# A MoE block's down projection with stationary weights, and three of twelve low parts made on GpSimd

## Chip, core and metric

The kernel runs on one core of one Trainium2 chip. The metric is the device time of one execution in microseconds, the median of three runs. The engines are called as the profile calls them: PE is TensorE's matmul, PEld its weight load, DVE is VectorE, ACT is ScalarE, POOL is GpSimd, and SP is the engine that issues most of the DMAs.

## What is computed

A decoder block over 512 tokens of width 1024: a gated linear recurrence and a sliding-window attention side by side, then a mixture of 32 experts of which every token takes four. The change touches the mixture alone. All is float32, and the weights of all 32 experts are read once, 12 MiB for each.

```python
def moe_ffn(h, w_router, b_router, w_up, b_up, w_down, b_down):
    logits = xf @ w_router + b_router
    top_vals, top_idx = lax.top_k(logits, 4)
    gates = softmax(top_vals)
    ...
    def expert_block(args):                    # xb: the tokens of one expert
        hu = xb @ w_up[e] + b_up[e]            # 1024 -> 2048
        x_glu = jnp.minimum(hu[:, ::2], 7.0)
        x_lin = jnp.clip(hu[:, 1::2], -7.0, 7.0)
        act = x_glu * sigmoid(1.702 * x_glu) * (x_lin + 1.0)
        return act @ w_down[e] + b_down[e]     # 1024 -> 1024
    ...                                        # times the gate, added to the token's row
```

## The kernel before

**Float32 by halves.** A float32 weight is cut into a float16 high part and a float16 low part, and so are the activations; a product is the sum of three float16 passes (high by high, high by low, low by high: `PASSES`). `split` does the cutting for one chunk of weights, 1 MiB as [128, 2048] float32: ACT writes the high part (line 344, a scaled copy), DVE writes the low part in one instruction (line 345: source times scale minus high part, both inputs in SBUF).

**One expert.** Up to C = 96 token slots are gathered into `xg` (`pick`), transposed, by matmuls with a one-hot matrix. The up projection takes eight chunks (`up_k`, line 1141): the weights are stationary, the 96 slots move, 48 matmuls to a chunk, into four PSUM banks `pu`. `swiglu` on DVE and ACT makes the activations in two halves: the first as float16 high and low parts (`act`), the second as float32 (`act32`). The down projection takes four chunks (`down_j`): here the activations are stationary and the weights move, 512 columns at a time, into two PSUM banks `pd`. Chunks 0 and 1 use float16 parts (line 1182, 24 matmuls); chunks 2 and 3 are used as float32 just as they were loaded (line 1176, 16 records), so they need no split. `finish` (line 1189) multiplies `pd` by the gate and a row of modulation on DVE, and POOL adds the rows to the output in DRAM by an indirect DMA (line 1190).

**Order.** The loop does the up projection of expert e, then the down projection of expert e-1, so that `swiglu` of e lies under the down projection. Each engine works in its program's order. Before each chunk i on PE, `ahead(i)` puts the splits of the chunks up to i + 6 into the programs of ACT and DVE, as far as slots are free. There are 18 slots of 1 MiB. At most 14 of them hold loaded chunks that wait for their split; four take turns for the cut parts (`slot_69`, `slot_68`, `slot_66` and `slotc_3547` in the order of instructions). So the high part of chunk m is written into the slot that PE has finished with at chunk m-4, and the next load into a staged slot is issued by SP when its split is over.

Of the kernel before, what the change touches and what calls it, by code (L numbers as in the profile page):

```python
# [10 lines left out]
F32 = mybir.dt.float32  # L11
F16 = mybir.dt.float16
# [29 lines left out]
def block_body(tc, x, c, positions, w_ada, b_ada, norm1_gain, w_in, lower_bound_logits, hg_norm_gain,  # L42
# [19 lines left out]
    with top:  # L62
# [44 lines left out]
        # ------------------------------------------------------------------ load order  # L107
# [88 lines left out]
        # ------------------------------------------------------------------ constants  # L196
# [52 lines left out]
        # ------------------------------------------------------------------ small vectors  # L249
# [7 lines left out]
        def rsqrt(dst, src, scale, tmp):  # L257
            """dst = (src * scale + eps) ** -0.5 by Newton steps from the exponent; tmp: as wide as dst"""
# [12 lines left out]
        # ------------------------------------------------------------------ x -> xn -> transposed  # L271
# [64 lines left out]
        def split(key, n, view_in=None, view_hi=None, keep=False):  # L336
            """cut a staged chunk of n columns into float16 high and low parts"""
# [7 lines left out]
            V.scalar_tensor_tensor(lo, src, SW, hi, op0=OP.mult, op1=OP.subtract)  # L345
# [8 lines left out]
        def rotary():  # L354
            # rotary angles, brought into [-pi, pi]
# [39 lines left out]
        # ------------------------------------------------------------------ first group: q, k, v of the attention  # L395
# [29 lines left out]
        # vectors that are not needed before this point  # L425
# [20 lines left out]
        # masks of the halving levels: mask_s[j, i] = same 2s-block, j in its lower half, i in its upper one  # L446
# [18 lines left out]
        # ------------------------------------------------------------------ attention  # L465
# [120 lines left out]
        # ------------------------------------------------------------------ HGRN2  # L586
# [49 lines left out]
            # decayed keys with the tokens on the partitions  # L636
# [48 lines left out]
        # ------------------------------------------------------------------ main stream of the input projection  # L685
# [8 lines left out]
        def gemm_T(key, half, bk):  # L694
            """128 columns of a chunk, transposed: [columns, tokens]"""
# [7 lines left out]
        def gemm_tok(key, t, dst, first):  # L703
            """256 columns of a chunk for one tile of tokens: [tokens, columns]"""
# [45 lines left out]
        # the other four modulation vectors, as rows of 512 on the partitions 0 and 32, then in DRAM  # L750
# [68 lines left out]
        # ------------------------------------------------------------------ branches, merged  # L819
# [62 lines left out]
        # rows of the modulation vectors on every partition: gate 1, shift 2, (1 + scale 2) * gain, gate 2  # L882
# [10 lines left out]
        def proj_out(t, c0, n):  # L893
            """columns c0 to c0 + n of a tile of tokens, in banks of 512"""
# [11 lines left out]
        # router weights as float16 high and low parts, and the row that does not depend on the token  # L906
# [39 lines left out]
        def logits(t, pieces):  # L946
            """pieces: (first column, columns) of the output projection"""
# [91 lines left out]
        def split_up(e, k):  # L1039
            split(("up", e, k), 2048, view_in=lambda t: t.rearrange("p (f g) -> p g f", g=2),  # L1040
                  view_hi=lambda t: t.rearrange("p (g f) -> p g f", g=2))
# [9 lines left out]
        def ahead(i):  # L1051
            while cut[0] < len(order) and cut[0] <= i + LOOK and free_slots:
# [3 lines left out]
                elif o[2] < 2:  # L1056
                    split(o, 2048)
# [326 lines left out]
```

## Time and profile before

| what | value |
|---|---|
| runs | 1550.11, 1550.6 and 1554.58 us, median 1550.6 |
| the profiled execution, first to last instruction | 1555.5 us |
| PE busy / PEld busy | 1457.5 us (94%) / 1050.4 us (68%) |
| DVE busy | 1264.8 us (81%) |
| ACT busy | 930.9 us (60%) |
| POOL busy | 127.9 us (8%) |
| HBM read and written | 463.49 MB and 14.70 MB |

The profile is of one execution. Its span is 0.3% over the median of the runs. The experts fill the span from about 500 us to its end; before that come the projections, the recurrence and the attention, which the change leaves alone. Busy time of PE is modelled, so that a busy PE isn't PE at its peak. Idle time of an engine is put down to the last thing it waited for.

### The profile page before, as it was taken

How to read it: one execution, taken by the hardware profiler on the slowest of the kernel's cores; microseconds unless marked ns; L12 is line 12 of the kernel's file. 1: busy time of each engine (PE TensorE's matmuls, PEld its weight loads, DVE VectorE, ACT ScalarE, POOL GpSimd, SP SyncE). 2: the span in 40 equal slices, each digit the busy share in tenths (PEclk: the TensorE clock that was granted, in tenths of full speed). 3: DMA queues.
4: the chain of work that ended last, by engine and by line, in shares of the span. 5: the costliest groups of instructions: out<-in, count | busy, mean ns of one | idle time of the engine just before them, and what ended most of it. 6: DMA issues, size and time to landing. Idle time of an engine off the chain costs nothing. (4 is left out here: it accounts for less than half of the span.)

```text
span 1555.5 us, 41689 instructions
## 1 busy us (share of the span) xinstructions
PE 1457.5 (94%) x18596; PEld 1050.4 (68%) x18596; DVE 1264.8 (81%) x1509; ACT 930.9 (60%) x827; POOL 127.9 (8%) x107
## 2 busy tenths in 40 slices
PE   3879999999969999999999999999999999999996
PEld 2545567444439777777877777877778777777872
DVE  7876577677798998877888887888888888888883
ACT  3356334523348776666767756767757777657761
POOL 4320000100020220000000000000000000000000
PEclk9899999999989999999999999999999999999998
DMA  9742311674848999999999999999999999999971
GB/s 283 221 128 75 100 37 55 207 248 151 339 177 331 359 391 405 380 380 352 381 380 392 396 391 388 382 385 388 391 392 385 386 397 392 383 385 382 390 260 14
DMA packets 121761, 476.73 MB, mean 306 GB/s; under 512 B 10733, under 2 KB 43594, under 8 KB 88746
## 3 DMA queue, kind: packets, MB, share of 16 engines
q1 hardware_dynamic: 114400, 459.04, 76.9%
q0 software_dynamic: 5440, 12.72, 3.9%
q8 instruction: 147, 2.41, 0.6%
q10 hardware_dynamic: 1738, 2.27, 0.4%
q14 instruction: 36, 0.29, 0.1%
HBM read 463.49 MB, written 14.70 MB: 307 GB/s over the span
## 5 line engine op out<-in xcount | busy, mean ns | idle before, releaser
L1141 PE MATMUL pu<-xg,slot 128*128 128x96 f16 x9264 | 422.1, 206 | 14.1 <-issue 10.5
L1141 PEld LDWEIGHTS <-slot 128*128 128x128 f16 x9264 | 405.0, 98 | 35.7 <-issue 30.9
L344 ACT ACTIVATE slot<-slot 128x2048 f16<-128x2048 f32 (+1 forms) x135 | 271.2, 2018 | 155.3 <-PE pu L1141 73.2
L345 DVE SCALAR_TENSOR_TENSOR slot<-slot,slot 128x2048 f16<-128x2048 f32 (+1 forms) x135 | 303.6, 2269 | 60.5 <-ACT slot L344 57.7
L345 DVE SCALAR_TENSOR_TENSOR slot<-slotb,slot 128x2048 f16<-128x2048 f32 x86 | 195.4, 2287 | 36.4 <-ACT slot L344 32.3
L344 ACT ACTIVATE slot<-slotb 128x2048 f16<-128x2048 f32 x86 | 176.6, 2066 | 72.5 <-PE pu L1141 60.5
L700 PE MATMUL mm<-hT,slot 128*128 128x512 f16 x672 | 153.2, 385 | 0.0
L344 ACT ACTIVATE slot<-slotc 128x2048 f16<-128x2048 f32 x47 | 94.5, 2034 | 88.9 <-PE pu L1141 75.0
L1190 POOL DMA_INDIRECT out_dram<-y,idx x32 | 63.5, 1984 | 1014.4 <-DVE y L1189 905.7
L1182 PEld LDWEIGHTS <-act 128*96 128x96 f16 x768 | 92.5, 124 | 78.8 <-issue 14.2
L345 DVE SCALAR_TENSOR_TENSOR slot<-slotc,slot 128x2048 f16<-128x2048 f32 x47 | 106.3, 2287 | 46.8 <-ACT slot L344 46.7
L1141 PE MATMUL pu<-xg,slotc 128*128 128x96 f16 x3024 | 138.8, 206 | 0.0
L1141 PEld LDWEIGHTS <-slotc 128*128 128x128 f16 x3024 | 132.0, 98 | 0.0
L1182 PE MATMUL pd<-slot,act 128*96 128x512 f16 x564 | 129.7, 384 | 0.2 <-issue 0.2
L700 PEld LDWEIGHTS <-slot 128*128 128x128 f16 x672 | 66.3, 99 | 78.1 <-issue 6.9
L1107 PE MATMUL gb<-sel,h 128*128 128x96 f16 x2048 | 109.4, 207 | 2.1 <-issue 1.3
L1107 PEld LDWEIGHTS <-h 128*128 128x128 f16 x2048 | 95.3, 98 | 3.3 <-issue 1.6
L1176 PE MATMUL pd<-slot,act 128*96 128x512 f32 x208 | 91.4, 592 | 0.0
L345 DVE SCALAR_TENSOR_TENSOR slotc<-slotb,slotc 128x2048 f16<-128x2048 f32 x36 | 82.2, 2284 | 1.2 <-ACT slotc L344 0.8
L344 ACT ACTIVATE slotc<-slotb 128x2048 f16<-128x2048 f32 x36 | 74.0, 2055 | 7.9 <-PE pu L1141 7.8
L345 DVE SCALAR_TENSOR_TENSOR slotc<-slot,slotc 128x2048 f16<-128x2048 f32 x34 | 77.6, 2283 | 0.7 <-ACT slotc L344 0.7
L344 ACT ACTIVATE slotc<-slot 128x2048 f16<-128x2048 f32 x34 | 70.1, 2063 | 4.1 <-PE pu L1141 3.0
(322 smaller groups left out, 1762.8 us busy)
## 6 DMA issues: line engine op xcount, KB each, us to landing
slot<-in_w_up_dram SPq DMA_DIRECT2D x117, 1024.0 KB, 10.0
slotb<-in_w_up_dram SPq DMA_DIRECT2D x101, 1024.0 KB, 9.1
slot<-in_w_down_dram SPq DMA_DIRECT2D x50, 1024.0 KB, 9.4
slotb<-in_w_down_dram SPq DMA_DIRECT2D x41, 1024.0 KB, 9.8
slotc<-in_w_up_dram SPq DMA_DIRECT2D x38, 1024.0 KB, 10.7
slotc<-in_w_down_dram SPq DMA_DIRECT2D x37, 1024.0 KB, 9.0
slot<-in_w_in_dram SPq DMA_DIRECT2D x16, 1024.0 KB, 7.5
slot<-in_w_ada_dram SPq DMA_DIRECT2D x16, 1024.0 KB, 7.1
```

Source lines behind the costliest of these rows:

```text
L344: A.activation(hi, src, AF.Copy, scale=SW)
L345: V.scalar_tensor_tensor(lo, src, SW, hi, op0=OP.mult, op1=OP.subtract)
L700: T.matmul(bk, lhsT=hl[:, o:o + 128], rhs=hT[:, ph, k, :], start=(k == 0 and n == 0), stop=(k == KT - 1 and n == 2))
L1107: T.matmul(bk[:, C * k:C * k + C], lhsT=h2[:, part, t, 128 * kk:128 * kk + 128], rhs=sel[:, t, :], start=(k == 0 and t == 0), stop=(t == N ...
L1141: T.matmul(o, lhsT=hl[:, 2048 * pw + 128 * f:2048 * pw + 128 * f + 128], rhs=xg[:, pa_, k, :], start=(k == 0 and f % 4 == 0 and n == 0), s ...
L1176: T.matmul(pd[u][:C, :], lhsT=act32[:, k - 4, :], rhs=w[:, o + 512 * u:o + 512 * u + 512], start=False, stop=(k == KT - 1))
L1182: T.matmul(pd[u][:C, :], lhsT=act[:, pa_, k, :], rhs=w[:, c0:c0 + 512], start=False, stop=False)
L1190: G.indirect_dma_start(out=out2, out_offset=bass.IndirectOffsetOnAxis(ap=idx[:C, :1], axis=0), in_=y[:C, :], in_offset=None, bounds_check= ...
```

## The change

**Down projection.** `down_j` makes the weights stationary and lets the 96 slots move, as `up_k` does: 48 matmuls of 96 columns to a chunk, 192 to an expert, all in float16 parts, with eight bias matmuls of 96 columns. The result lies transposed in `pd`. `take_down` copies it to SBUF, one bank by ACT and one by DVE; `finish` turns it back with eight float32 transposes on PE into two banks `gb`, and DVE multiplies from there. `finish` of an expert now runs after the first chunk of the up projection that follows. `swiglu` makes high and low parts of both halves.

**Splits.** All twelve chunks of an expert are cut now, ten before. ACT makes all twelve high parts, DVE nine low parts. Three low parts (up chunks 1 and 5, down chunk 1) go to POOL: one instruction multiplies the loaded chunk by the scale in place, a second subtracts the high part. The first eight chunks of all stay on DVE.

```diff
-        def split(key, n, view_in=None, view_hi=None, keep=False):
+        def split(key, n, view_in=None, view_hi=None, low=None):
...
             A.activation(hi, src, AF.Copy, scale=SW)
-            V.scalar_tensor_tensor(lo, src, SW, hi, op0=OP.mult, op1=OP.subtract)
+            if low is G:
+                G.tensor_scalar(st[:, :n], st[:, :n], SW, None, op0=OP.mult)
+                G.tensor_sub(lo, src, hi)
+            else:
+                V.scalar_tensor_tensor(lo, src, SW, hi, op0=OP.mult, op1=OP.subtract)
...
                 o = order[cut[0]]
+                low = G if cut[0] >= 8 and (o[0], o[2]) in ON_POOL else V
                 if o[0] == "up":
-                    split_up(o[1], o[2])
-                elif o[2] < 2:
-                    split(o, 2048)
+                    split_up(o[1], o[2], low)
+                else:
+                    split(o, 2048, low=low)
...
+            glu(0)
+            lin(0)
+            high(0)
+            glu(1)
+            lin(1)
+            low(0)
+            high(1)
+            low(1)
...
         def down_bias(eb):
-            for u in range(2):
-                T.matmul(pd[u][:C, :], lhsT=eb, rhs=bd[:, 512 * u:512 * u + 512], start=True, stop=False)
...
+            for f in range(8):
+                T.matmul(pd[f // 4][:, C * (f % 4):C * (f % 4) + C], lhsT=bd[:, 128 * f:128 * f + 128], rhs=eb,
+                         start=(f % 4 == 0), stop=False, skip_group_check=True)
...
+        def down_j(w, j, act):
             for k in (2 * j, 2 * j + 1):
...
-                if k >= 4:
-                    for u in range(2):
-                        T.matmul(pd[u][:C, :], lhsT=act32[:, k - 4, :], rhs=w[:, o + 512 * u:o + 512 * u + 512],
-                                 start=False, stop=(k == KT - 1))
-                    continue
-                for n, (pa_, pw) in enumerate(PASSES):
-                    for u in range(2):
-                        c0 = 2048 * pw + o + 512 * u
-                        T.matmul(pd[u][:C, :], lhsT=act[:, pa_, k, :], rhs=w[:, c0:c0 + 512], start=False,
-                                 stop=False)
...
+                for f in range(8):
+                    o = pd[f // 4][:, C * (f % 4):C * (f % 4) + C]
+                    for n, (pa_, pw) in enumerate(PASSES):
+                        c0 = 2048 * pw + 1024 * (k % 2) + 128 * f
+                        T.matmul(o, lhsT=w[:, c0:c0 + 128], rhs=act[:, pa_, k, :], start=False,
+                                 stop=(k == KT - 1 and n == 2), skip_group_check=True)
+
+        def take_down():
+            yt = moe.tile([128, KT, C], F32, name="yt")
+            A.activation(yt[:, 0:4].rearrange("p k c -> p (k c)"), pd[0][:, :4 * C], AF.Copy)
+            V.tensor_copy(yt[:, 4:8].rearrange("p k c -> p (k c)"), pd[1][:, :4 * C])
+            return yt
...
+        def finish(yt, gate, idx):
             y = moe.tile([128, D], F32, name="y")
             for u in range(2):
+                bk = pse.tile([128, 512], F32, name="gb", bufs=2)
+                for f in range(4):
+                    T.transpose(bk[:C, 128 * f:128 * f + 128], yt[:, 4 * u + f, :], ident)
                 sl = slice(512 * u, 512 * u + 512)
-                V.scalar_tensor_tensor(y[:C, sl], pd[u][:C, :], gate[:C], g2row[:C, sl], op0=OP.mult, op1=OP.mult)
+                V.scalar_tensor_tensor(y[:C, sl], bk[:C, :], gate[:C], g2row[:C, sl], op0=OP.mult, op1=OP.mult)
...
+ON_POOL = (("up", 1), ("up", 5), ("dn", 1))
```

POOL's program where the experts begin, before: after the last gathering of `h` it holds one indirect DMA for each expert and nothing else.

```order
L1002 TENSOR_TENSOR h_2309<-xa,h_2309 128x1024
L1190 DMA out_dram<-y,idx 512x1024 x32
```

The same place now, with what each instruction waits for. The chunk that POOL multiplies lies in a staged slot, and each low part goes into `slot_68`, every fourth turn of the four slots.

```order
L1006 TENSOR_TENSOR h_2309<-xa,h_2309 128x1024 [waits Activation_49]
L346 TENSOR_SCALAR slot_67<-slot_67 128x2048 [waits DMAHW6_49,DMAHW2_49,Activation_49]
L347 TENSOR_TENSOR slot_68<-slot_67,slot_68 128x2048 [waits DVE_49,DMAHW7_49,PE_49,Pool_49]
L346 TENSOR_SCALAR slot_64<-slot_64 128x2048 [waits DMAHW6_49,Activation_49]
L347 TENSOR_TENSOR slot_68<-slot_64,slot_68 128x2048 [waits PE_49,Pool_49]
L346 TENSOR_SCALAR slotb_2881<-slotb_2881 128x2048 [waits DMAHW3_49,DMAHW2_49,Activation_49]
L347 TENSOR_TENSOR slot_68<-slotb_2881,slot_68 128x2048 [waits PE_49,Pool_49]
L346 TENSOR_SCALAR slotb_2885<-slotb_2885 128x2048 [waits DMAHW6_49,DVE_49,Activation_49]
L347 TENSOR_TENSOR slot_68<-slotb_2885,slot_68 128x2048 [waits PE_49,Pool_49]
L1222 DMA out_dram<-y,idx 512x1024 [waits DMASW4_49,DMASW5_49,DMASW3_49,DMASW6_49,DMASW2_49,DVE_49]
```

So POOL gets 94 pairs of a multiply and a subtract in all, and the indirect DMA stands in line between them.

DVE's program around the end of one expert, before: splits (line 345) and `swiglu`, then the two instructions of `finish`, which read `pd`.

```order
L345 SCALAR_TENSOR_TENSOR slot_68<-slotb_2885,slot_68 128x2048
L1160 SCALAR_TENSOR_TENSOR act<-sg_l,act 128x384
L1156 TENSOR_TENSOR act_11075<-act_11075,sg_s 128x384
L345 SCALAR_TENSOR_TENSOR slot_66<-slot_70,slot_66 128x2048
L345 SCALAR_TENSOR_TENSOR slotc_3547<-slot_67,slotc_3547 128x2048
L1129 COPY ebc<-E_2948 64x96
L1189 SCALAR_TENSOR_TENSOR y<-pd_3559,gate,g2row 96x512
L1189 SCALAR_TENSOR_TENSOR y<-pd_3560,gate,g2row 96x512
```

The same place now:

```order
L349 SCALAR_TENSOR_TENSOR slot_66<-slotb_2884,slot_66 128x2048
L1178 SCALAR_TENSOR_TENSOR act<-sg_l,act 128x384
L1173 TENSOR_TENSOR sg_l<-sg_l,sg_s 128x384
L349 SCALAR_TENSOR_TENSOR slotc_3547<-slotb_2885,slotc_3547 128x2048
L1178 SCALAR_TENSOR_TENSOR act<-sg_l,act 128x384
L349 SCALAR_TENSOR_TENSOR slot_69<-slot_70,slot_69 128x2048
L1211 COPY yt<-pd_3560 128x384
L1221 SCALAR_TENSOR_TENSOR y<-gb,gate,g2row 96x512 x2
```

The splits into `slot_68` are gone from DVE's program, and a second low part of the activations and the copy of `pd` have come in.

## Rows read from the trace of the kernel before

**Rows 1.** The page's head: span and instructions of the execution.

```profile
span 1555.5 us, 41689 instructions
```

**Rows 2.** Busy time, clock and DMA of three stretches among the experts.

```profile
core 0: us, PE busy (x) PEld busy (x) DVE busy (x) ACT busy (x) POOL busy (x), PEclk, DMA share, GB/s
1015.00:1025.00 10.00, 9.96 (x134) 7.53 (x134) 8.90 (x14) 7.39 (x6) 0.00 (x0) 1.00 1.03 415
860.00:990.00 130.00, 128.32 (x2032) 101.29 (x2031) 111.86 (x103) 90.33 (x67) 5.68 (x4) 1.00 1.00 390
990.00:1120.00 130.00, 127.69 (x2026) 100.70 (x2025) 111.19 (x95) 90.31 (x66) 5.68 (x4) 1.00 1.00 385
```

**Rows 3.** POOL's timeline, two of 32 output DMAs: start, length, instruction, idle before.

```profile
595.95 1.43 POOL L1190 DMA_INDIRECT out_dram<-y,idx  x1 [31.11 <-DVE y L1189]
...
1465.97 1.42 POOL L1190 DMA_INDIRECT out_dram<-y,idx  x1 [31.18 <-DVE y L1189]
```

**Rows 4.** Waits from 990 to 1120 us: total, times, longest; the second is SP's.

```profile
ACT slot L344 <- PE pu L1141: 35.2, 13, 7.2
...
SPq L160 <- DVE slot L345: 50.6, 12, 6.4
```

**Rows 5.** PE's timeline from an expert's last up chunk to the next expert's first.

```profile
1016.99 2.20 PE L1141 MATMUL pu<-xg,slot 128*128 128x96 f16 x48
1019.12 0.85 PE L1134 MATMUL pu<-ebc,bu 64*128 64x96 f16 x16
1019.82 0.59 PE L1169 MATMUL pd<-bd,ebc 64*96 64x512 f16 x2
...
1025.56 7.03 PE L1176 MATMUL pd<-slotb,act 128*96 128x512 f32 x16
1032.42 1.78 PE L1141 MATMUL pu<-xg,slot 128*128 128x96 f16 x38
```

**Rows 6.** DVE's timeline in that expert: splits, a step of `swiglu`, `finish`.

```profile
1007.73 6.69 DVE L345 SCALAR_TENSOR_TENSOR slot<-slotc,slot 128x2048 f16<-128x2048 f32 x3
...
1022.28 0.55 DVE L1155 SCALAR_TENSOR_TENSOR sg_l<-sg_l,sg_g 128x384 f32<-128x384 f32 x1
...
1031.81 1.56 DVE L1189 SCALAR_TENSOR_TENSOR y<-pd,gate,g2row 96x512 f32<-96x512 f32 x2
```

**Rows 7.** Groups by line, 1000 to 1130 us: busy, mean ns, idle before.

```profile
L344 ACT ACTIVATE slot<-slot 128x2048 f16<-128x2048 f32 x15 | 30.7, 2063 | 16.2 <-PE pu L1141 14.8 <-DMA slotc<-in_w_down_dram 0.6 <-PE pd L1182 0.6
```

**Rows 8.** Timelines of DVE and of POOL at four places where both work.

```profile
25.49 1.76 DVE L345 SCALAR_TENSOR_TENSOR slot<-slot,slot 128x1536 f16<-128x1536 f32 x1
...
25.49 3.08 POOL L300 TENSOR_TENSOR acc1p<-slot,cs 128x768 f32<-128x768 f32 x1 [0.86 <-PE tp L320]
...
27.16 1.96 DVE L332 TENSOR_TENSOR hT<-h,hT 128x512 f16<-128x512 f32 x1
...
291.50 2.60 DVE L768 SCALAR_TENSOR_TENSOR acc<-slot,cs,acc 128x1024 f32<-128x1024 f32 x2
...
293.00 0.25 POOL L924 IOTA iota_c<- 128x128 f32 x1
...
438.80 2.12 POOL L1002 TENSOR_TENSOR h<-xa,h 128x1024 f16<-128x1024 f32 x1 [6.72 <-ACT h L1001]
...
439.23 0.24 DVE L981 SCALAR_TENSOR_TENSOR lg<-sd,rs,brow 128x32 f32<-128x32 f32 x1
...
452.75 2.12 POOL L1002 TENSOR_TENSOR h<-xa,h 128x1024 f16<-128x1024 f32 x1 [8.14 <-ACT h L1001]
...
452.84 2.04 DVE L1006 TENSOR_TENSOR gt<-tv 128x4 f32<-128x4 f32 x1
```

**Rows 9.** POOL's two-input instructions by line: shortest, median and longest ns.

```profile
L302 POOL TENSOR_TENSOR acc1p<-acc1p x16: 721/784/2324, 17.6 to 68.9; 128x256 f32<-128x256 f32 x16
...
L300 POOL TENSOR_TENSOR acc1p<-slot,cs x8: 1465/1532/3084, 16.0 to 65.1; 128x768 f32<-128x768 f32 x8
...
L1002 POOL TENSOR_TENSOR h<-xa,h x4: 2120/2122/2272, 429.3 to 464.2; 128x1024 f16<-128x1024 f32 x4
```

**Rows 10.** Float32 transposes on PE, 395 to 470 us, by line.

```profile
L967 PE MATMUL sd<-ident,xa 128*128 128x128 f32 x32 | 5.5, 292 | 4.0 <-DVE xa L960 1.7 <-DVE gs L1008 1.3 <-DVE aux L1013 0.9
```

More of the change, by code (lines that the diff above doesn't have):

```diff
@@ L1144, in block_body, with swiglu, glu, lin @@
         SU = SW * SH2
[L1146 removed]
+        def swiglu(act):
             n = 4 * C
[L1148 to L1160 removed]
+            gs_, ls_, ss_ = [], [], []
+            def glu(hf):
+                g = moe.tile([128, n], F32, name="sg_g", bufs=2)
+                s = moe.tile([128, n], F32, name="sg_s")
+                V.tensor_scalar(g, pu[hf][:, :n], 1.0 / SU, 7.0, op0=OP.mult, op1=OP.min)
+                A.activation(s, g, AF.Sigmoid, scale=1.702)
+                gs_.append(g)
+                ss_.append(s)
+            def lin(hf):
+                l = moe.tile([128, n], F32, name="sg_l", bufs=2)
+                V.tensor_scalar(l, pu[2 + hf][:, :n], -7.0 * SU, 7.0 * SU, op0=OP.max, op1=OP.min)
+                V.scalar_tensor_tensor(l, l, SU, gs_[hf], op0=OP.add, op1=OP.mult)
+                ls_.append(l)
+            def parts(hf):
+                return (act[:, q, 4 * hf:4 * hf + 4].rearrange("p k c -> p (k c)") for q in range(2))
+            def high(hf):
+                V.tensor_mul(ls_[hf], ls_[hf], ss_[hf])
+                A.activation(next(parts(hf)), ls_[hf], AF.Copy, scale=SACT / SU)
+            def low(hf):
+                hi, lo = parts(hf)
+                V.scalar_tensor_tensor(lo, ls_[hf], SACT / SU, hi, op0=OP.mult, op1=OP.subtract)
+            glu(0)
[6 more added lines that the diff above has]
+            low(1)
@@ L1252, in block_body @@
         i = 0
+        left = None
         for e in range(NEX + 1):
@@ L1263, in block_body @@
                     i += 1
+                    if k == 0 and left:
+                        finish(*left)
                 up_bias(eb)
-            if e < NEX:
                 for _ in prep:
@@ L1268, in block_body @@
                 acts[e] = new_act()
-                for hf_ in range(2):
-                    swiglu(hf_, *acts[e])
+                swiglu(acts[e])
             if e > 0:
+                if e == NEX:
+                    finish(*left)
                 _, gate, idx, eb = state.pop(e - 1)
@@ L1276, in block_body @@
                     key = ("dn", e - 1, j)
[L1277 to L1282 removed]
+                    down_j(hlmap[key], j, acts[e - 1])
+                    hl_done(key)
                     i += 1
[L1284 removed]
+                left = (take_down(), gate, idx)
                 acts.pop(e - 1)
+            if e == NEX:
+                finish(*left)
             if e == 0:
@@ L1330, in block_body @@
             up_bias(eb)
-            for hf_ in range(2):
-                swiglu(hf_, act, act32)
+            swiglu(act)
             down_bias(eb)
```

46 lines of the change are left out of this document (9 added, 37 removed).

## The prediction

> **What bounds the kernel now.** I read the length of an expert first, then the busy times in the steady stretch, then the waits, then the timelines of single engines. An expert's output DMA starts 26 times between 595.95 and 1465.97 us [rows 3], so an expert takes 870.02 / 26 = 33.46 us. In 260 us of that stretch PE is busy for 256.0, DVE for 223.1 and ACT for 180.6 us [rows 2]: per expert 32.9, 28.7 and 23.2 us. POOL has little else than its output DMA. The DMA share is 1.00 at 385 to 390 GB/s [rows 2]. So two resources are full at once, PE and the DMA engines. Which one leads is told by the waits: ACT waits 35.2 of 130 us for PE to hand back a slot, and SP waits for DVE's splits before it may load [rows 4]. The pressure runs from PE to ACT to DVE to SP: PE leads, and the DMA engines are close behind. DVE has 33.46 - 28.7 = 4.8 us to spare, and that is the number on which this change turns.
>
> **The down projection on PE.** Now it lasts from the bias at 1019.82 to the next up chunk at 1032.42, 12.6 us, of which the float32 chunks are 7.03 us [rows 5]. After the change a chunk is 48 matmuls of the form that an up chunk has, and such a chunk takes 1019.12 - 1016.99 = 2.13 us from start to start [rows 5]. Four make 8.5 us; eight bias matmuls at 2.13 / 48 add 0.4; eight float32 transposes at 5.5 / 32 = 0.17 us [rows 10] add 1.4. Together 10.3 us, so PE gains 2.3 us per expert and would need 31.2 us. The DMA engines would set the next floor: 33.46 us at 388 GB/s is 12.97 MB, and at the 415 GB/s of the best 10 us shown [rows 2] this takes 31.3 us. So the edit on PE could give 2.2 us per expert if nothing else became late.
>
> **ACT.** Two more high parts at 2.06 us [rows 7], half of the copy of the result, and one more small step, each taken at the 0.55 us of a [128, 384] instruction [rows 6]: 23.2 + 4.1 + 1.1 = 28.4 us. This is below 33.46 and stays off the path.
>
> **DVE.** A split costs 6.69 / 3 = 2.23 us back to back [rows 6]. One goes (ten to nine); a low part of the activations and a copy of the result come, 0.55 us each [rows 6]: 28.7 - 2.2 + 1.1 = 27.6 us of its own work. By this alone DVE would fit.
>
> **POOL's three parts.** Before, POOL does nothing in these stretches that DVE could feel, so the price of sharing has to come from the early phases. There the rows are plain [rows 8]. At 25.49 a split on DVE (1.76 us) and a two-input instruction on POOL start together; POOL's lasts 3.08 us in place of the 1.465 us that the shortest of its kind takes [rows 9], so it waited until the split was over. At 27.16 DVE's next instruction finds POOL at work and takes 1.96 us. At 452.84 a subtraction of four columns takes 2.04 us, because POOL began a 2.12 us instruction just before it. So an instruction on either engine keeps the other out for its whole length, when DVE reads two operands from SBUF and POOL reads from SBUF. Two rows show the limits: a DVE instruction with one operand in PSUM (`sd`) goes through in 0.24 us at 439.23 under POOL's work, and POOL's iota, which reads nothing, goes through at 293.00 under a DVE instruction of two inputs [rows 8].
>
> The subtract of a part has the types of L1002, 2.12 us for 1024 columns [rows 9]. From L302 and L300 (0.721 us for 256 columns, 1.465 for 768) the fixed part is 0.35 us and a column costs 1.45 ns [rows 9]. For 2048 columns that gives 3.33 us by the float32 lines, 0.35 + 2 x 1.77 = 3.90 by L1002, and 4.24 if L1002 is simply doubled. I take 3.90, from the line with the same types. The multiply reads one operand and no row shows one on POOL: between half the price per column, 0.35 + 2048 x 0.73 ns = 1.84 us, and the price of a subtract. I take 1.84, since it reads half as much. A part is 5.74 us and three are 17.2 us per expert. The Trainium skill (GPSIMD Engine Reference, 3.1 and 4.1) measures a two-input instruction of 2048 float32 columns at 4.5 us on GpSimd and calls one-input ones roughly line-rate, and advises VectorE for such work; with 4.5 for the subtract the sum below would be 1.8 us per expert higher.
>
> **The sum.** DVE's 27.6 us hold 4.3 us that read PSUM (four steps of `swiglu` and the copy at 0.55, `finish` at 1.56 [rows 6]) and may lie under POOL's work. If none of them does, an expert takes 27.6 + 17.2 = 44.8 us; if all do, 40.5. DVE works in program order, so what lies next to a POOL instruction is chance; I take the middle, 42.7 us. This is above PE's 31.2, ACT's 28.4 and the DMA floor of 31.3, so their gains lie idle. A second path gives about the same: every POOL part goes into the same one of the four result slots, so that slot's lap holds ACT's 2.06, POOL's 5.74 and PE's 2.13, 9.9 us, with up to two waits of 2.23 us for a split on DVE 14.4; three laps make an expert, 30 to 43 us. Behind a late low part PE stands with all later matmuls. SP's issue of the next load into that slot waits for POOL too, with the loads behind it; the cover is the 14 staged slots, more than an expert's twelve chunks, and in a slower loop the DMA engines have time to catch up. POOL's output DMA waits behind a pair, 5.7 us at most, and its buffer is wanted again only an expert later: nothing.
>
> POOL has 94 pairs, 94 / 3 = 31.3 experts' worth. 31.3 x (42.7 - 33.46) = 289 us. The sum is a difference against the profiled execution of 1555.5 us [rows 1], which is 0.3% over the median; I add it to the median: 1550.6 + 289 = 1840 us.
>
> **Rivals.**
> 1. *Faster: POOL's work runs beside DVE's.* The exclusion of [rows 8] would not hold for these instructions, or POOL's share would be far smaller. It decides at a hold of (33.46 - 27.6) / 3 = 2.0 us per part without any overlap with the PSUM steps, 3.4 us with all of it; below that DVE still fits in 33.46 us. Then PE's gain counts down to the DMA floor: 31.3 x 2.2 = 69 us, 1482 us. For it: no row among the experts shows POOL computing beside a split. Against: the split at 25.49 is the very instruction of line 345, and even the cheapest price of the subtract alone is 3.33 us.
> 2. *Slower, but the multiply does not exclude.* Only two-input instructions on POOL would; the rows show just these. Then 3 x 3.90 = 11.7 us are added: 35.0 to 39.3, middle 37.2 us per expert, 1550.6 + 31.3 x 3.7 = 1667 us. The Trainium skill (SBUF — State Buffer, "Who interferes with whom") states that a DVE instruction with two SBUF inputs contends with any GpSimd instruction that reads SBUF, and that the one that starts first keeps the other out to its end. By that rule the multiply excludes as well and this rival falls; the trace agrees for two-input instructions [rows 8], and no row here shows a one-input one.
> 3. *Much slower: the multiply costs as much as a subtract.* At 4.24 us each, 25.4 us are added: 48.7 to 53.0, middle 50.9 us, 1550.6 + 31.3 x 17.4 = 2095 us. Nothing in the rows prices a column of one input.
> 4. *No change.* The hold falls by chance between rival 1 and 2 (a little over 3 us per part), and PE's gain pays for it.
>
> **How the numbers follow.** Forecast 0.75, rival 1 0.06, rival 2 0.10, rival 3 0.07, rival 4 0.02. The forecast's own range comes from the ends of the subtract and of the overlap: 23.3 + 3 x 5.17 = 38.8 us to 27.6 + 3 x 6.08 = 45.8 us per expert, 1718 to 1937 us. To hold 8 in 10 it takes in rival 2 from somewhat below its middle, and a little at the upper end for idle time of DVE that no sum holds: 1640 to 1950 us. Rivals 1, 3 and 4 are left out. A run of this kernel can tell about 0.3% from no change. Faster by more than that 0.06, within it 0.02, slower by more 0.92.
>
> **What would show it.** In the profile after, among the experts: an output DMA every 42 to 43 us; POOL busy for 40% or more; instructions of line 349 on DVE longer than 2.3 us, many by one POOL instruction's length; PE idle with its releaser on POOL's line 347 or DVE's 349; DMA share near 0.75 and some 305 GB/s. The step on PE is right if a down projection's 192 matmuls take 8 to 9 us where nothing waits. The prediction is wrong if the splits on DVE keep their 2.23 us while POOL works, or if POOL's pairs take less than 3.4 us.

## The result and the profile after

The changed kernel takes 2197.74 us (median of four runs, 2189.36 to 2202.49) beside 1550.36 us for the kernel before: the ratio is 1.4159, with a 95% interval of 1.41 to 1.4217. The direction was as predicted; the size was not, 2198 us against 1840 and a range that ended at 1950.

The head of the page of the changed kernel answers to [rows 1]; busy time, granted clock and DMA share over the whole span follow it. The last four lines are groups by line: busy us and mean ns of one, then the idle time before them and what ended most of it.

```profile
span 2200.7 us, 52954 instructions
...
PE 1555.9 (71%) x23908; PEld 1345.2 (61%) x23908; DVE 1684.3 (77%) x1543; ACT 1071.5 (49%) x955; POOL 1210.3 (55%) x295
...
PEclk9999999988888888888888788888888888888877
DMA  9521166666666666666666565666666666666640
...
L1146 PE MATMUL pu<-xg,slot 128*128 128x96 f16 x9168 | 549.5, 232 | 366.3 <-POOL slot L347 355.2
...
L346 POOL TENSOR_SCALAR slot<-slot 128x2048 f32<-128x2048 f32 x41 | 256.6, 6258 | 239.8 <-ACT slot L344 239.7
...
L349 DVE SCALAR_TENSOR_TENSOR slot<-slot,slot 128x2048 f16<-128x2048 f32 (+1 forms) x111 | 278.0, 2504 | 81.1 <-ACT slot L344 78.2
...
L347 POOL TENSOR_TENSOR slot<-slot,slot 128x2048 f16<-128x2048 f32 x41 | 200.4, 4887 | 3.4
```

No engine is full now. PE stands 355.2 us for POOL's low parts in one group alone, and the DMA engines, full in [rows 2], are at six tenths. POOL in turn waits 239.7 us in one group for ACT's high part. A circle of waits is the sign that no engine's own work sets the time.

The output DMAs on POOL's timeline answer to [rows 3]: start, length, instruction, and idle time before it.

```profile
612.17 3.36 POOL L1222 DMA_INDIRECT out_dram<-y,idx  x1 [0.16 <-issue]
...
2071.43 3.36 POOL L1222 DMA_INDIRECT out_dram<-y,idx  x1
```

Between these two lie 27 experts: 1459.26 / 27 = 54.05 us for each, where there were 33.46. The first ten take 52.5 us each (612.17 to 1137.44), the next seventeen 54.9. The forecast was 42.7, and 31.3 experts at 54.05 - 42.7 make 355 us: the whole miss lies in the loop over the experts.

**The price that failed** is read from two answers by line: shortest, median and longest duration in ns of POOL's multiply and of its subtract.

```profile
L346 POOL TENSOR_SCALAR slot<-slot x41: 5363/5372/10808, 484.7 to 2146.6; 128x2048 f32<-128x2048 f32 x41
...
L347 POOL TENSOR_TENSOR slot<-slot,slot x41: 4049/4252/11001, 490.1 to 2152.3; 128x2048 f16<-128x2048 f32 x41
```

The multiply, which reads one operand, takes 5.37 us where nothing disturbs it. The subtract, which reads two, takes 4.05. The prediction gave 1.84 and 3.90.

**One circle of the result slot** shows what the time is made of. The rows are from the timelines of one expert, 1032 to 1085 us: first POOL's, then ACT's, then PE's.

```profile
1053.76 5.37 POOL L346 TENSOR_SCALAR slot<-slot 128x2048 f32<-128x2048 f32 x1 [5.66 <-ACT slot L344]
1059.21 4.72 POOL L347 TENSOR_TENSOR slot<-slot,slot 128x2048 f16<-128x2048 f32 x1
1069.76 10.35 POOL L346 TENSOR_SCALAR slotc<-slotc 128x2048 f32<-128x2048 f32 x1 [5.82 <-ACT slot L344]
1080.19 4.24 POOL L347 TENSOR_TENSOR slot<-slotc,slot 128x2048 f16<-128x2048 f32 x1
```

```profile
1051.76 1.91 ACT L344 ACTIVATE slot<-slot 128x2048 f16<-128x2048 f32 x1 [5.95 <-PE pu L1146]
...
1067.56 2.11 ACT L344 ACTIVATE slot<-slotc 128x2048 f16<-128x2048 f32 x1 [0.31 <-issue]
```

```profile
1032.14 6.58 PE L1146 MATMUL pu<-xg,slot 128*128 128x96 f16 x95 [8.40 <-POOL slot L347]
...
1048.15 3.44 PE L1146 MATMUL pu<-xg,slot 128*128 128x96 f16 x47 [3.95 <-POOL slot L347]
...
1063.99 5.81 PE L1205 MATMUL pd<-act,slot 128*128 128x96 f16 x95 [3.49 <-POOL slot L347]
...
1084.48 1.78 PE L1146 MATMUL pu<-xg,slot 128*128 128x96 f16 x20 [8.39 <-POOL slot L347]
```

Read them in order of time; the rows leave the numbers of the slots out, and POOL's three low parts all go into `slot_68`. PE gets a chunk at 1048.15 and is through with it at 1051.6. Only then may ACT write the next high part into that slot (1051.76). POOL multiplies (1053.76) and subtracts (1059.21 to 1063.93), and PE starts the next chunk of that slot at 1063.99: 15.8 us for a lap. The lap after it takes 20.5 us, to 1084.48, in the main because the multiply of 1069.76 needs 10.35 us in place of 5.37. The lap before, from 1032.14 to 1048.15, takes 16.0 us. There are three laps to an expert, and these three make 52.3 us: the laps fill this expert's time.

**Why that multiply is long** is in DVE's timeline at the same time. The first two rows lie under the subtract of 1059.21, the last two under the multiply of 1069.76 and the subtract behind it.

```profile
1060.07 0.54 DVE L1158 TENSOR_SCALAR sg_g<-pu 128x384 f32<-128x384 f32 x1
1060.53 3.42 DVE L1126 TENSOR_TENSOR gate<-gate 96x1 f32<-96x1 f32 x1
...
1075.27 5.25 DVE L349 SCALAR_TENSOR_TENSOR slotc<-slotb,slotc 128x2048 f16<-128x2048 f32 x1
1080.44 1.40 DVE L1221 SCALAR_TENSOR_TENSOR y<-gb,gate,g2row 96x512 f32<-96x512 f32 x2
```

A multiplication of a single column on DVE lasts 3.42 us, to the end of POOL's subtract; a step of `swiglu` that reads PSUM passes in its own 0.54 us just before it, and so do the two steps of the finish (0.70 us each). This is the exclusion of [rows 8], and POOL's one-input multiply keeps DVE out as well: the split of 1075.27 takes 5.25 us. The Trainium skill (SBUF — State Buffer, "Who interferes with whom") says the same, that a DVE instruction with two SBUF inputs contends with any GpSimd instruction that reads SBUF; the trace agrees. POOL can lose as well, and several times in a row: while its multiply stood from 1069.76, DVE went through two splits and two short steps.

**The granted clock** is the last part of a lap: PE busy, DMA share and clock of three single chunks.

```profile
1048.15:1051.43 3.28, 3.28 (x48) 3.28 (x49) 3.28 (x2) 0.00 (x0) 0.00 (x0) 0.58 0.67 210
1052.11:1054.15 2.04, 2.04 (x53) 2.04 (x51) 0.34 (x1) 1.94 (x2) 0.39 (x1) 1.00 0.99 398
1063.99:1067.40 3.41, 3.41 (x49) 3.41 (x50) 3.41 (x7) 0.94 (x2) 0.00 (x0) 0.58 0.63 213
```

The columns are those of [rows 2]. The chunk after each of these two waits of PE is granted 0.58, mostly the lower level of 1.2 GHz, and takes 3.3 to 3.4 us; the one at 1052.11 runs at 1.00, the level of 2.4 GHz, in 2.04 us. The wait thus adds 1.2 to 1.4 us to the lap that caused it. After the longer wait of 8.40 us, at 1032.14, two chunks take 6.42 us, 2.3 more than at 1.00.

### The profile page after: what moved, and what is told of

The parts are those of the page before. It is cut to its first block, busy times and chain, and to the rows that moved or that the text cites. A ratio compares the mean times of both kernels' runs of the same rounds, so it can differ in the third digit from the quotient of the medians.

```text
span 2200.7 us, 52954 instructions
## 1 busy us (share of the span) xinstructions
PE 1555.9 (71%) x23908; PEld 1345.2 (61%) x23908; DVE 1684.3 (77%) x1543; ACT 1071.5 (49%) x955; POOL 1210.3 (55%) x295
## 5 line engine op out<-in xcount | busy, mean ns | idle before, releaser
L1146 PE MATMUL pu<-xg,slot 128*128 128x96 f16 x9168 | 549.5, 232 | 366.3 <-POOL slot L347 355.2
L1146 PEld LDWEIGHTS <-slot 128*128 128x128 f16 x9168 | 521.4, 114 | 379.9 <-POOL slot L347 365.1
L346 POOL TENSOR_SCALAR slot<-slot 128x2048 f32<-128x2048 f32 x41 | 256.6, 6258 | 239.8 <-ACT slot L344 239.7
L346 POOL TENSOR_SCALAR slotb<-slotb 128x2048 f32<-128x2048 f32 x40 | 254.2, 6355 | 238.8 <-ACT slot L344 236.0
L1205 PE MATMUL pd<-act,slot 128*128 128x96 f16 x4656 | 257.8, 227 | 176.4 <-POOL slot L347 163.5
L1205 PEld LDWEIGHTS <-slot 128*128 128x128 f16 x4656 | 247.7, 110 | 179.0 <-POOL slot L347 167.9
L347 POOL TENSOR_TENSOR slot<-slot,slot 128x2048 f16<-128x2048 f32 x41 | 200.4, 4887 | 3.4
L1131 DVE TENSOR_TENSOR sel<-iota_c,pos 128x384 f16<-128x384 f32 x32 | 84.7, 2648 | 147.1 <-PE gb L1117 147.1
L347 POOL TENSOR_TENSOR slot<-slotb,slot 128x2048 f16<-128x2048 f32 x40 | 187.8, 4695 | 3.3
L349 DVE SCALAR_TENSOR_TENSOR slot<-slotc,slot 128x2048 f16<-128x2048 f32 x55 | 153.5, 2791 | 40.9 <-ACT slot L344 40.9
L349 DVE SCALAR_TENSOR_TENSOR slotc<-slot,slotc 128x2048 f16<-128x2048 f32 x40 | 151.3, 3783 | 4.1 <-ACT slotc L344 4.1
L346 POOL TENSOR_SCALAR slotc<-slotc 128x2048 f32<-128x2048 f32 x13 | 81.7, 6288 | 75.0 <-ACT slot L344 57.5
```

Source lines behind the costliest of these rows:

```text
L346: G.tensor_scalar(st[:, :n], st[:, :n], SW, None, op0=OP.mult)
L347: G.tensor_sub(lo, src, hi)
L1131: V.tensor_tensor(sel, iota_c[:, None, :C].to_broadcast([128, NT, C]), pos[:, :, e:e + 1].to_broadcast([128, NT, C]), op=OP.is_equal)
L1146: T.matmul(o, lhsT=hl[:, 2048 * pw + 128 * f:2048 * pw + 128 * f + 128], rhs=xg[:, pa_, k, :], start=(k == 0 and f % 4 == 0 and n == 0), s ...
L1205: T.matmul(o, lhsT=w[:, c0:c0 + 128], rhs=act[:, pa_, k, :], start=False, stop=(k == KT - 1 and n == 2), skip_group_check=True)
```

## Experiments

Two theories stood against each other: that DVE and POOL keep each other out, so that DVE's work and POOL's add up (the exclusion, theory X in the expectations), and that the lap of the one result slot sets the pace (theory L). Times per expert are the median distance of the output DMAs of ten of the first experts, unless the text says otherwise. Where no ratio is given, the kernel was run once; the half multiply was run twice (ratio 1.3372).

**The two halves of the change apart.** First without POOL: all twelve low parts on DVE.

```diff
-ON_POOL = (("up", 1), ("up", 5), ("dn", 1))
+ON_POOL = ()
```

> The changed kernel with all twelve low parts on DVE; POOL keeps only the output DMA. Both theories blame POOL's parts for the loss, so both expect it to vanish. DVE then has 27.6 us of own work plus three splits at 2.23 us, 34.3 us per expert, which is more than the 31.2 us of PE and the 31.3 us of the DMA engines: 34.3 us per expert, 1550 + 31.3 x (34.3 - 33.46) = 1577 us, 1560 to 1600. If the new down projection itself were at fault, the time would stay over 1800 us.

Measured 1610.23 us, ratio 1.0372 (1.0332 to 1.0411), a little above the expected 1560 to 1600. An expert takes 33.65 us, later 35.7. Here is the stretch from 610 to 975 us, with the columns of [rows 2]:

```profile
610.00:975.00 365.00, 328.58 (x7319) 319.06 (x7316) 364.26 (x326) 299.03 (x230) 182.59 (x11) 1.00 1.00 383
```

PE falls from the 98% of [rows 2] to 90%: the new down projection does make it cheaper. DVE is busy 364.26 of 365 us and takes the lead, so the gain shows nowhere. The DMA engines are full too, but SP, which issues the loads, waits 268 of the 365 us for DVE's splits and never for a transfer. The later experts cost most of the 60 us.

Then POOL's three parts alone, with the down projection of the kernel before, so that ten chunks of an expert are cut.

```diff
-                        T.matmul(o, lhsT=w[:, c0:c0 + 128], rhs=act[:, pa_, k, :], start=False,
-                                 stop=(k == KT - 1 and n == 2), skip_group_check=True)
+                        T.matmul(pd[u][:C, :], lhsT=act[:, pa_, k, :], rhs=w[:, c0:c0 + 512], start=False,
+                                 stop=False)
...
```

> The kernel before with its own down projection and ten splits, of which the same three low parts go to POOL. Theory X: DVE's 28.7 - 3 x 2.23 = 22.0 us plus POOL's holds of 3 x 8.1 = 24.3 us, 42 to 46.3 us per expert, 1815 to 1950 us. Theory L: laps as in the changed kernel, 50 to 54 us, 2070 to 2200 us. If POOL's parts hurt only together with the new down projection, 1550 to 1600 us.

Measured 2044.4 us, between the two expectations; an expert takes 47.5 to 52 us. DVE is busy only 203.41 of 260 us (78%), so it is not DVE's sum that leads; the laps of this kernel were not measured. POOL's parts alone cost 494 us, where the whole change costs 647.

**The multiply, in four ways.** Left out (the low parts of three chunks are then made from unscaled weights):

```diff
-                G.tensor_scalar(st[:, :n], st[:, :n], SW, None, op0=OP.mult)
```

> The changed kernel without POOL's multiply; the low parts of the three chunks are then wrong, the subtract is there. It prices the multiply. Theory L (the lap of the one result slot that all POOL parts use: PE's chunk, ACT's high part, multiply, subtract, PE again) takes 5.45 us off each of three laps: 54.4 - 16.4 = 38.0 us per expert, 1685 us. Theory X (the exclusion of DVE and POOL, as a sum) expects 27.6 + 3 x 4.06 = 39.8 us, or 35.5 with all overlap: 1605 to 1740 us. The forecast's price of 1.84 us for a multiply would leave the time above 2000 us.

Made by ACT:

```diff
-                G.tensor_scalar(st[:, :n], st[:, :n], SW, None, op0=OP.mult)
+                A.activation(st[:, :n], st[:, :n], AF.Copy, scale=SW)
```

> The changed kernel with the multiply of the three chunks on ACT, in place, after the high part; POOL only subtracts. ACT then has 28.4 + 3 x 2.06 = 34.6 us per expert. Theory X (exclusion as a sum): 27.6 us of DVE plus three subtracts of 4.06 us, 39.8 us, as without the multiply: 1750 to 1830 us. Theory L (the lap of the one result slot): ACT's pass stands in the lap in place of POOL's, 3 x 2.06 us more than without the multiply: 1850 to 1980 us.

Over half of the columns (the other half stays unscaled):

```diff
-                G.tensor_scalar(st[:, :n], st[:, :n], SW, None, op0=OP.mult)
+                G.tensor_scalar(st[:, :n // 2], st[:, :n // 2], SW, None, op0=OP.mult)
```

> The changed kernel with GpSimd's multiply over the first 1024 of the 2048 columns of a chunk (the other half of these three chunks stays unscaled). Theory (the multiply keeps VectorE out for nearly its own length): the multiply lasts about half of 5.37 us, say 2.8, and an expert costs half of the multiply's 12.8 us less: about 46 us in the first experts, 1950 to 2030 us in all. Rival (the price lies in the extra hop through GpSimd, its order and its semaphores, not in the columns): 52 to 54 us per expert as in the changed kernel, 2130 us or more.

And on POOL, but as a two-input instruction with a broadcast column of the scale:

```diff
-                G.tensor_scalar(st[:, :n], st[:, :n], SW, None, op0=OP.mult)
+                G.tensor_mul(st[:, :n], st[:, :n], swc[:, 0:1].to_broadcast([128, n]))
```

> The changed kernel with POOL's multiply by a scalar written as a two-input multiply with a broadcast column. It asks what makes the multiply dear. If the form of the instruction does, the two-input one costs 0.35 + 2048 x 1.45 ns = 3.3 us by the lines of the kernel before, 2.0 us less in each lap: theory L 2010 us; theory X, which counts the hold (about 4.0 us of the 5.37, now 3.3), 2130 us. If 2048 columns of float32 in place cost 5.4 us in any form, 2180 to 2220 us.

| multiply | us | us per expert, first experts | its undisturbed length |
|---|---|---|---|
| on POOL (the change) | 2197.7 | 52.5 | 5.37 |
| left out | 1786.4 | 39.8 | - |
| on ACT | 1816.0 | 40.7 | 1.91 (ACT) |
| POOL, half the columns | 2074.3 | 47.8 | 2.77 |
| POOL, two inputs | 2121.6 | 53.2 | 3.60 |

The stretch from 700 to 960 us, the multiply left out, then made by ACT:

```profile
700.00:960.00 260.00, 217.95 (x4522) 211.82 (x4520) 249.54 (x171) 181.00 (x137) 152.31 (x27) 0.93 0.88 329
```

```profile
700.00:960.00 260.00, 208.78 (x4320) 200.81 (x4320) 244.23 (x174) 211.77 (x156) 109.43 (x26) 0.95 0.90 319
```

Without POOL's multiply DVE is busy for 96% and 94% and leads. There the upper end of the exclusion's sum fits: DVE's 27.6 us and three subtracts of 4.06 make 39.8, measured 39.8. DVE's timeline from 700 to 745 us bears it out: the three subtracts there lie against splits and the making of `sel`, and of the steps that read PSUM only one lies under a subtract. In its total the kernel without the multiply lies above both expectations, in part since its later experts took 40.9 us; the one with the multiply on ACT lies where the exclusion put it. The multiply on POOL costs 52.5 - 39.8 = 12.7 us per expert, 4.2 for each; the half multiply gives 4.7 of these back, somewhat less than half, so most of the price goes with the columns and not with an extra step through POOL. In its total the half multiply missed what the exclusion expected, in the main because its later experts took 51 to 56 us. The two-input form tells most. Two rows by line (shortest, median, longest), multiply and subtract:

```profile
L348 POOL TENSOR_TENSOR slot<-slot,swc x41: 3594/3601/9090, 487.2 to 2066.0; 128x2048 f32<-128x2048 f32 x41
...
L349 POOL TENSOR_TENSOR slot<-slot,slot x41: 4085/5957/6007, 490.9 to 2070.0; 128x2048 f16<-128x2048 f32 x41
```

The multiply is 1.77 us shorter, and the median subtract 1.7 us longer (5.96 against 4.25): it now waits for a split of DVE, and the pair is as long as it was, 9.6 us. For DVE nothing changes: a split that waits gets in 3.47 us after the start of this multiply, and 3.50 us after the start of the longer one (the last section shows how this is read). That is why the first experts gained nothing. The later ones take 49.5 us here, where the changed kernel has 54.6; this brings the total near the 2130 us of the exclusion, and its cause was not followed up.

**The lap.** Two slots go from the loaded chunks to the cut ones, six result slots in place of four, so that POOL's parts don't share one.

```diff
-        more_slots(moe, "slotc", NSC, NS + NSB + NSC - NH)
+        more_slots(moe, "slotc", NSC, NS + NSB + NSC - NH - 2)
```

> The changed kernel with six result slots in place of four (two fewer for loaded chunks). POOL's work and DVE's are the same; a high part may be written two chunks earlier. Theory L: the lap spans six chunks, so two laps make an expert and the slot no longer binds; POOL's own 31.9 us and PE set the time, 32 to 36 us per expert, 1500 to 1630 us. Theory X: 47.5 to 51.9 us per expert from DVE's 27.6 us and POOL's measured holds of three times about 8.1 us, 1980 to 2120 us.

Measured 2055.32 us, 46.7 us per expert in the first experts and 49.6 later. The stretch from 700 to 960 us of the changed kernel, then with six slots:

```profile
700.00:960.00 260.00, 177.05 (x3322) 171.33 (x3320) 212.45 (x132) 137.62 (x104) 186.91 (x35) 0.83 0.65 246
```

```profile
700.00:960.00 260.00, 197.18 (x3926) 191.02 (x3923) 246.82 (x145) 151.38 (x117) 206.61 (x41) 0.84 0.75 278
```

DVE goes from 82% to 95%. The total lies where the exclusion put it, the time per expert a little below its 47.5. So both theories are right, in layers: the lap holds the changed kernel at 52.5 us, and when it is widened, the exclusion holds it at 46.7. With DVE at 95%, more slots alone can hardly bring it near the kernel before.

In the third lap ACT's high parts stand behind its copy of the result, which waits for PE. To see whether that matters, DVE made both copies.

```diff
-            A.activation(yt[:, 0:4].rearrange("p k c -> p (k c)"), pd[0][:, :4 * C], AF.Copy)
+            V.tensor_copy(yt[:, 0:4].rearrange("p k c -> p (k c)"), pd[0][:, :4 * C])
```

> The changed kernel with the copy of both banks of the down projection on DVE; ACT makes none, so its next high part no longer stands behind the end of a down projection. Theory L: one lap in three loses ACT's wait of 4.5 us: about 50 us per expert, 2065 us. Theory X: DVE gets 0.5 us more: 2200 to 2215 us.

Measured 2323.18 us, outside both. The first experts took 51.4 us, 1.1 less than in the changed kernel, so that wait is a small part of the loss. The later ones took 64.9. In 260 us of them DVE is busy for 136.3, and the copy of `ebc` in DVE's program, with the splits behind it, stands up to 16.2 us for PE's bias matmuls of the down projection. The order of the later experts' programs changes in this kernel as in the changed one; whether that made them so slow was not tested.

**Towards a better kernel.** The first run had shown that PE's gain is real and that DVE lacks time for it. So DVE's work has to shrink without POOL. With no part on POOL, chunks 2 and 3 of the down projection as float32, stationary, ten splits:

```diff
-                    split(o, 2048, low=low)
+                elif o[2] < 2:
+                    split(o, 2048, low=low)
...
+                    if k >= 4:
+                        c0 = 1024 * (k % 2) + 128 * f
+                        T.matmul(o, lhsT=w[:, c0:c0 + 128], rhs=act32[:, k - 4, :], start=False,
+                                 stop=(k == KT - 1), skip_group_check=True)
+                        continue
```

> Weights stationary in the down projection, POOL without splits, and down chunks 2 and 3 again used as float32 as they were loaded (16 float32 matmuls of 96 columns to a chunk), so that ten splits are left. DVE: 34.3 - 2 x 2.23 = 29.8 us per expert; PE: 31.2 us plus about 0.5 us for each of two chunks, 32.2 us; DMA engines 31.3 us. If DVE is what holds the kernel without POOL parts (theory of DVE's load), 32.2 to 32.6 us per expert: 1510 to 1525 us. If PE's gain was never real, 33.5 us and 1550 us or more.

Measured 1593.14 us, ratio 1.0267 (1.0225 to 1.0308), 34.0 us per expert and 35.3 later. PE is busy for 248.81 of 260 us and leads: a float32 chunk with stationary weights costs it 3.7 us (32 records of 0.115 us), not the 2.6 that was expected. The time is the one expected if PE's gain was never real, but this price explains it: the 30.3 us that PE is busy per expert without POOL, and 1.65 us more for each of two chunks, make 33.6. With only the last chunk as float32, eleven splits, and both copies of the result on ACT:

```diff
-                elif o[2] < 2:
+                elif o[2] < 3:
...
-                    if k >= 4:
+                    if k >= 6:
...
-            V.tensor_copy(yt[:, 4:8].rearrange("p k c -> p (k c)"), pd[1][:, :4 * C])
+            A.activation(yt[:, 4:8].rearrange("p k c -> p (k c)"), pd[1][:, :4 * C], AF.Copy)
```

> The changed kernel without GpSimd's parts, with only the last chunk of the down projection used as float32 (stationary weights), and both copies of the result on ScalarE. Eleven splits on VectorE. Theory (each engine's own work decides): VectorE 33.65 us per expert without GpSimd, less one split (2.23) and one copy (0.55), plus a half step (0.3): 31.2 us. TensorE 34.0 us with two float32 chunks of 3.7 us each, less 1.65 for one of them: 32.4 us, which leads. With some loss in the later experts, as every variant so far showed, 1525 to 1560 us: level with the kernel before or a little faster. Rival (the lap of the four result slots, now with eleven chunks through it in place of ten, holds the loop, whatever the engines need): 34.0 us or more in the first experts and 1590 us or more in all.

Measured 1567.92 us, ratio 1.0105 (1.0071 to 1.0138), just above the expected 1525 to 1560. The first fifteen experts take 32.3 us, as worked out, the later ones 34.7. At the same place the order of the programs changes. In the first experts DVE makes all splits of one down projection before `swiglu` of the next expert; in the later ones two splits stand between the first steps of `swiglu`, where there were none, and one between the two steps of the finish. The last experiment of this line holds the first order throughout, by edges of order alone (`lows` and `highs` keep the instructions that write the low and the high part of a chunk):

```diff
-                swiglu(*acts[e])
+                with tc.issue_after(lows[("dn", e - 1, 2)].ins):
+                    swiglu(*acts[e])
...
-                    if k in PICK_AT:
+                    if k == 7 and e > 0:
+                        with tc.issue_after(lows[("dn", e - 1, 2)].ins):
+                            next(prep, None)
+                    elif k in PICK_AT:
...
-                        finish(*left)
+                        with tc.issue_after(lows[("up", e, 3)].ins):
+                            finish(*left)
...
-                left = (take_down(), gate, idx)
+                with tc.issue_after(highs[("up", e + 1, 3)].ins):
+                    left = (take_down(), gate, idx)
```

> The kernel of the run before (eleven splits, no part on GpSimd, one float32 chunk), with the order of the first experts held through all of them: the activations' first step behind the third split of the down projection, the copies of the result behind the fourth high part of the next up projection, the finish behind its fourth low part. In that run an expert took 32.2 us up to the sixteenth and 34.7 us after it, where the order of VectorE's and ScalarE's programs changes. Theory (the order is what costs the 2.5 us): 32.2 to 32.8 us per expert throughout, so some 15 experts by 2 to 2.5 us less than 1568: 1528 to 1540 us, faster than the kernel before by about 1%. Rival (something else sets in with the later experts, the memory or the clock, and the order only follows): 34 us or more in the later experts again, 1560 to 1570 us.

Measured 1528.59 us, ratio 0.985 (0.9826 to 0.9874): this kernel beats both. Two stretches of the run before and two of this one:

```profile
700.00:960.00 260.00, 252.39 (x5308) 249.15 (x5306) 249.16 (x233) 209.90 (x170) 25.35 (x8) 1.00 1.01 399
1200.00:1460.00 260.00, 242.06 (x4943) 231.98 (x4940) 234.76 (x216) 193.26 (x157) 37.96 (x7) 1.00 0.98 371
```

```profile
700.00:960.00 260.00, 253.07 (x5328) 249.93 (x5326) 250.94 (x234) 210.62 (x170) 26.04 (x8) 1.00 1.01 401
1200.00:1460.00 260.00, 252.55 (x5289) 248.45 (x5286) 248.21 (x229) 206.21 (x169) 43.40 (x8) 1.00 1.01 397
```

With the order held, the later stretch is as full as the first: PE 97%, DVE 95%, the DMA engines all of the time at about 400 GB/s. An expert takes 32.5 us there, and 31.7 in the first ten. The gain over the kernel before is about 1 us per expert, less than the 2.2 us that the floor of the best 10 us in [rows 2] had promised; at 400 GB/s the 12.97 MB of an expert take 32.4 us. SP now waits for transfers too, 58.5 us of the later stretch, so the memory's pace comes in; PE at 97% is as near its end, and which of the two holds is not shown.

**The order in the changed kernel.** It was held in the same way.

```diff
-                swiglu(acts[e])
+                with tc.issue_after(lows[("dn", e - 1, 2)].ins):
+                    swiglu(acts[e])
...
-                left = (take_down(), gate, idx)
+                with tc.issue_after(highs[("up", e + 1, 2)].ins), tc.issue_after(lows[("up", e + 1, 2)].ins):
+                    left = (take_down(), gate, idx)
```

> The changed kernel as it is, with the order of VectorE's and ScalarE's programs in the first experts held through all of them, in the same way as in the run before. Theory (the order costs the later experts their rise from 52.6 to about 55 us here too, and the rest of the excess is GpSimd's price): 52.6 us per expert throughout, some 17 experts by 2.5 us less than 2197.7: 2145 to 2170 us. Rival A (the later experts are slower because TensorE falls to the lower clock after its waits, whatever the order): 54 to 55 us per expert again, 2185 to 2205 us. Rival B (the order is the larger part of the excess over the forecast of 42.7 us): clearly below 52.6 us per expert already in the first experts, under 2100 us.

Measured 2208.37 us, ratio 1.4252 (1.4193 to 1.4312). The first experts take 52.5 us as before, the later ones 55.7, although DVE's order stays the same but for one short step. So DVE's order is not what makes the later experts of the changed kernel slower. The time lies just above what the rival on the clock gave, but the granted clock in the later stretch is 0.81 after 0.84, which alone doesn't prove it. The gathering of the next expert's tokens still moves to another place in this kernel, on ACT. What costs these 2 to 3 us per expert stays open.

## Why the prediction came out as it did

**The bound and the spare time of DVE.** Right. DVE's 4.8 us to spare were the number on which the change turned: without POOL it is full to the last per cent with its share of the new work, and with POOL it is held up.

**The down projection on PE.** Right in size: 48 matmuls take 2.04 us where the clock is at its upper level, and PE's busy share falls without POOL. In the changed kernel it can't be seen, since PE waits and then runs at the lower level.

**The exclusion.** Right in kind: it was read from four rows of the early phases, and the trace after shows it for the subtract and for the multiply. Rival 1 (POOL beside DVE) and rival 2 (the multiply doesn't exclude) fall. "For its whole length" is right for the subtract, which keeps a split of DVE out for 4.0 to 4.1 us, nearly all of its 4.05 to 4.25. It is wrong for the multiply, which keeps one out for 3.5 of its 5.37 us.

**The price of the multiply.** This is the step that failed. "I take 1.84, since it reads half as much" was a guess about what sets POOL's pace. It is 5.37 us, three times as much, and even the stated upper bound, the price of a subtract (4.24 us), lay below it. What DVE feels of it, 3.5 us, is nearly twice the forecast too. The subtract was right: 3.90 against 4.05 us.

**Which path leads.** The price stood in two places, and the second is where it hurt. The lap was worked out as ACT's 2.06, POOL's 5.74 and PE's 2.13 us, 9.9 to 14.4 us, and called about the same as the sum. With the true lengths, 2.06 + 5.37 + 4.06 + 2.13, a lap is 13.6 us, 18.1 with two waits for DVE, and three are 41 to 54 us: mostly above the forecast, and around the 52.5 measured. The lap takes a part's whole length, while DVE is only held for some of it. PE's 2.13 us in that sum held no term for the clock; after a wait the chunk takes 3.3 to 3.4 us.

The miss then divides as follows, per expert. The forecast was 42.7. With six slots, where DVE leads, it is 46.7: 4.0 us are DVE's sum with the dear multiply. The prediction's own sum, with three holds of 3.5 and 4.1 us, gives 46.1 to 50.4. The four-slot lap adds 5.8, to 52.5. How much of this is the clock's was not measured: with six slots the granted clock is as low, 0.84 beside 0.83. The later experts bring the mean to 54.05, 1.5 us whose cause is open. With 5.37 us put into the sum as a hold, it would give 51.6 to 55.9 us per expert and a time near 2185 us, close to the measured one, but by luck: the kernel with six slots has the same multiplies and takes 46.7. Rival 3, a multiply as dear as a subtract at 2095 us, was nearest, but was given 0.07 and left out of the range.

**SP and the transfers.** Nothing to correct there: no wait for a transfer stands among the long ones. The DMA share of 0.6 is a consequence of the pace, lower than the forecast's 0.75 as the pace is.

## What to carry to other kernels

When the trace has no row for an instruction, a price made from half of another instruction's is a guess, and the range must reach well beyond the nearest row on the dear side; here one input cost more than two. Before giving work to an engine that keeps another busy one out, add up both paths with the same prices: the sum of the work that can't overlap, and the lap of the buffer that the slow engine now writes, in which its whole length counts. Where the steady pace shifts in the middle of an unrolled loop, compare the engines' programs on either side of the shift: holding the better order may be worth as much as the change itself.

## What the runs showed of the hardware

- A multiply of 2048 float32 columns by a constant, in place, takes POOL 5.37 us, and 2.77 us for 1024 columns, 2.5 ns per column. The same multiply written with two inputs, the second a broadcast column, takes 3.60 us. The Trainium skill (GPSIMD Engine Reference, 4.1) calls one-input work on GpSimd roughly line-rate; the trace disagrees.
- The multiply's hold on DVE ends before its recorded end. In the changed kernel a multiply stands from 1038.39 to 1043.77 us. A split begun at 1040.90 ends at 1044.19; by its own 2.28 us it got in at 1041.91, which is 3.52 us after the multiply's start and 1.86 us before its end (the rows are below). Read in this way, all 26 splits that wait under an undisturbed multiply between 600 and 2100 us get in after 3.49 to 3.52 us. The two-input multiply lets them in after 3.46 to 3.47 of its 3.60 us (26 of 26), the subtract of the changed kernel after 4.03 to 4.14 us (38 of 38).

```profile
1038.39 5.38 POOL L346 TENSOR_SCALAR slotb<-slotb 128x2048 f32<-128x2048 f32 x1 [2.80 <-ACT slot L344]
...
1040.90 3.29 DVE L349 SCALAR_TENSOR_TENSOR slot<-slot,slot 128x2048 f16<-128x2048 f32 x1 [6.66 <-ACT slot L344]
```

- In the kernel with two float32 chunks, the record of a stationary float32 weight load of 128x128 lasts 192 ns where a float16 one lasts 98 ns. Two records belong to a float32 matmul (2048 for 64 chunks of 16), and records overlap: 64 float32 ones took 7.22 us from 861.25. Line 1205 is the float32 chunk, line 1210 the float16 one:

```profile
L1205 PEld LDWEIGHTS pd<-act,slot x832: 187/192/192, 620.2 to 1580.2; 128*128 128x128 f32 x167
...
L1210 PEld LDWEIGHTS <-slot x2256: 95/98/99, 509.7 to 1573.2; 128*128 128x128 f16 x188
```
